# The first FFN of a macaron decoder layer in two token parts, each with seven products in place of eight

## The chip, the cores and the metric

The kernel runs on one core of a Trainium2 chip. The time is the device time of one execution in microseconds (us), the median of several runs; a profiled execution is recorded beside them. The engines are TensorE (PE in the profile; PEld is its weight load), VectorE (DVE), ScalarE (ACT), GpSimd (POOL) and SyncE (SP), which here issues the DMAs in one queue, in order.

## The reference

One decoder layer is computed on 1024 prompt tokens and 8 x 8 sample tokens, 1088 in all, with a model width of 1024. It is a macaron: half an FFN, a mixer (forgetting attention beside gated linear attention), half an FFN, each with a norm before and after.

```python
def rmsnorm(x, g):
    y = x32 * lax.rsqrt(jnp.mean(x32 * x32, axis=-1, keepdims=True) + NORM_EPS)
    return (y * g.astype(jnp.float32)).astype(x.dtype)

def swiglu(x, w_gu, w_down):
    gate, up = jnp.split(x @ w_gu, 2, axis=-1)
    return (jax.nn.silu(gate) * up) @ w_down

def macaron_half(x, g_pre, w_gu, w_down, g_post):
    return x + 0.5 * rmsnorm(swiglu(rmsnorm(x, g_pre), w_gu, w_down), g_post)
...
        hp = macaron_half(hp, ffn1_norm_pre[l], ffn1_w_gu[l], ffn1_w_down[l], ffn1_norm_post[l])
        fq, fk, fv, lf, gq, gk, gv, gg, la = project(rmsnorm(hp, mix_norm_pre[l]), w_in[l],
                                                     b_forget[l], w_gate_up[l], b_gate[l])
```

The FFN is 2752 wide. Behind the first FFN the result h is normalised again (`mix_norm_pre`) and multiplied by `w_in`: that is the projection.

## The kernel before, in words

**Layout.** Everything is kept transposed: 128 partitions are 128 of the model's or the FFN's features, and tokens run along the free dimension. The width of 1024 is 8 feature blocks (KB). Tokens come in four chunks, `CH` = (0,256), (256,256), (512,256), (768,320), written as (first, count); `MID` joins the first two to (0,512). HALF is 512, H1N the other 576.

**Precision.** A float32 operand is split in a high and a low part (`split`, L194 on ACT for the high part, L195 on DVE for the low one), and a product is three matmuls: high by high, high by low, low by high. Activations stand split in `ua` (first 512 tokens) and `ub` (last 576). A weight comes by DMA into a raw tile (`wr`, L118 in `Feed`, up to `ahead` of them split early), and its parts are `wh` and `wl`.

**The FFN.** Its 2752 columns are 22 blocks of 128 for gate and for up; block 0 is the odd one, whose half gate and half up share one weight. `GROUPS` cuts them in seven groups, [0,1], [2..5], [6..9], [10..13], [14..17], [18,19], [20,21], called G[0] to G[6]. For each block, gate and up are products over the chunks (`gemm`, L265, into PSUM tiles `mm`), DVE and ACT make silu(gate) x up and split it into `hh` and `hl`, and after a group `down` (L497) multiplies it back onto the 8 feature blocks of y, where DVE adds (L507) or, for G[0], ACT copies (L505). A group is planned as "first" (chunk after chunk as the norms come), "mid", or "final" (behind its downs stands the closing norm of each chunk, `after`). The first FFN is one `Part`, f1, over all 1088 tokens: G[0] first, G[1] to G[4] mid, and G[5] with G[6] final, once for the first 512 tokens and once for the others.

**Seven products.** The second FFN's second half (f3, 576 tokens) is planned with "sevens" already. Gate and up of one block are then seen as a product of 2 x 2 quarters: two halves of the 1024 features by two halves of the tokens, for the two weights. `seven` (L552) makes one product of half the features (4 x 3 matmuls) by half the tokens, and 7 of them give what 8 give in the plain way. It needs sums of weights, made by POOL (`Sums.load`: four DMAs L86, adds L89 and L94), sums of activations t1 to t4, made once by DVE and split, and additions of partial results on DVE (`job_seven`, L567 and L577). The sums of weights need scratch, given by `old`, and t1 to t4 need room, given by `room`.

**Norms.** `norm` (L351) sums squares (sq by ACT, ss by DVE or POOL, L275, L279, L281), adds over partitions on PE (`ncol`, L294), takes the power on DVE and POOL (`nv`, L324, L325), spreads it by a diagonal (`dg`, L336) and a matmul (`nrows`, L343), and multiplies: L382 for the closing norm, whose sum with x is L383 and is stored to `h1` by L388, and L405 for the next norm, split by L407 and L408 into `ua` or `ub`.

**Order.** A scheduler builds each engine's order from the program's. Each engine works in its own order, and so does SP's queue.

## Time and profile before

| what | value |
|---|---|
| median of three runs | 2387.77 us (2387.45 to 2388.52) |
| profiled execution, its own time | 2397.51 us |
| its span in the trace | 2395.8 us |
| mean granted TensorE clock | 0.984 |
| first product of the first FFN | 15.68 us |
| first product of the third chunk (`ub`) | 44.24 us |
| first product of the projection | 802.59 us |

The trace gives the start of every instruction in us, how long it took, its engine, its line, and the tiles that it writes and reads; in brackets stands how long the engine had been idle, and who ended that. A row of a window gives the stretch, its length, then for PE, PEld, DVE, ACT and POOL the busy time and, in brackets, the instructions; then the granted clock, the DMA share and GB/s. A closer look at the first FFN: from 200 to 300 us PE is busy for 100.00 us and DVE for 26.11.

### The profile page before, as it was taken

The page shows a single profiled execution, that of the slowest core. Times are in us where ns is not written, and L with a number is a line of the kernel's source. Part 1 is how long each engine was busy: PE and PEld are TensorE (multiplying, and loading weights), DVE is VectorE, ACT ScalarE, POOL GpSimd, SP SyncE. Part 2 cuts the span into 40 slices and gives each one's busy share as a digit, 9 for nine tenths or more (in the row PEclk, how much of TensorE's full clock was granted, in tenths as well). Part 3 has the DMA queues.
Part 4 walks back from the last instruction along what each step waited for, and adds up shares of the span by engine and source line. Part 5 has one row for each costly group of instructions (what it writes and reads, how often), then busy time and mean ns, then how long its engine had stood idle before and what let it go on. Part 6 is the DMA issues. An engine that isn't in the chain of part 4 may idle for free. (4 is left out here: it accounts for less than half of the span.)

```text
span 2395.8 us, 39346 instructions
## 1 busy us (share of the span) xinstructions
PE 2297.4 (96%) x15200; PEld 2041.2 (85%) x15200; DVE 1293.7 (54%) x2453; ACT 903.4 (38%) x1622; POOL 488.2 (20%) x514
## 2 busy tenths in 40 slices
PE   7999999999999999899998999998997999999997
PEld 6999999999989879899997666667786988999997
DVE  7223232232347774676465333339785696777765
ACT  5421211111134455755454222226565544334332
POOL 4000000000003230011124554531110224333402
PEclk9999999999999999999999999999998999999998
DMA  3211111111125576664458998766555544223212
GB/s 124 71 45 45 45 44 45 45 45 45 45 97 158 167 222 193 202 189 135 131 171 252 331 320 289 249 184 168 163 167 146 188 136 159 89 93 102 80 58 84
DMA packets 182267, 330.55 MB, mean 138 GB/s; under 512 B 25729, under 2 KB 101314, under 8 KB 182082
## 3 DMA queue, kind: packets, MB, share of 16 engines
q1 hardware_dynamic: 170418, 289.77, 38.8%
q0 software_dynamic: 11664, 38.28, 4.7%
q8 instruction: 120, 1.97, 0.3%
q14 instruction: 65, 0.53, 0.1%
HBM read 284.29 MB, written 43.69 MB: 137 GB/s over the span
## 5 line engine op out<-in xcount | busy, mean ns | idle before, releaser
L265 PE MATMUL mm<-ua,wh 128*128 128x512 f32 (+2 forms) x2288 | 635.4, 364 | 4.2 <-ACT ua L407 1.4
L265 PE MATMUL mm<-ub,wh 128*128 128x256 f32 (+2 forms) x2624 | 546.2, 303 | 10.7 <-ACT ub L194 8.3
L195 DVE TENSOR_TENSOR wl<-wr,wh 128x1024 fp32r<-128x1024 f32 (+1 forms) x258 | 312.0, 1210 | 337.7 <-ACT wh L194 325.7
L194 ACT CAST wh<-wr 128x1024 fp32r<-128x1024 f32 (+1 forms) x258 | 263.5, 1022 | 567.9 <-PE mm L265 196.8
L265 PEld LDWEIGHTS mm<-ua,wh 128*128 128x128 f32 (+1 forms) x2288 | 399.9, 191 | 80.7 <-issue 22.8
L265 PEld LDWEIGHTS mm<-ub,wh 128*128 128x128 f32 (+1 forms) x2624 | 428.3, 192 | 17.8 <-ACT ub L194 8.5
L265 PE MATMUL mm<-ua,wl 128*128 128x512 f32 (+1 forms) x1136 | 405.3, 358 | 1.2 <-DVE wl L195 1.2
L265 PE MATMUL mm<-ub,wl 128*128 128x256 f32 (+1 forms) x1296 | 386.8, 299 | 0.3 <-DVE wl L195 0.3
L497 PE MATMUL mm<-hl,wh 128*128 128x256 f32 (+2 forms) x1088 | 347.2, 320 | 0.8 <-DVE hl L195 0.5
L497 PE MATMUL mm<-hh,wh 128*128 128x256 f32 (+2 forms) x1040 | 337.1, 325 | 4.1 <-DVE y L507 2.0
L497 PE MATMUL mm<-hh,wl 128*128 128x256 f32 (+2 forms) x1040 | 331.9, 320 | 1.0 <-issue 1.0
L265 PEld LDWEIGHTS mm<-ub,wl 128*128 128x128 f32 x1296 | 248.4, 192 | 0.5 <-DVE wl L195 0.5
L265 PEld LDWEIGHTS mm<-ua,wl 128*128 128x128 f32 x1136 | 216.3, 191 | 33.3 <-DVE wl L195 2.3
L507 DVE TENSOR_TENSOR y<-y,mm 128x256 f32<-128x256 f32 (+2 forms) x272 | 130.1, 502 | 181.7 <-PE mm L497 169.5
L497 PEld LDWEIGHTS mm<-hl,wh 128*128 128x128 f32 x1088 | 205.9, 189 | 13.8 <-issue 2.0
L279 POOL TENSOR_TENSOR ss<-ss,sq 128x256 f32<-128x256 f32 (+1 forms) x46 | 46.1, 1003 | 836.9 <-ACT sq L275 836.3
L497 PEld LDWEIGHTS mm<-hh,wh 128*128 128x128 f32 x1040 | 196.0, 189 | 23.3 <-issue 6.5
L497 PEld LDWEIGHTS mm<-hh,wl 128*128 128x128 f32 x1040 | 196.4, 189 | 12.7 <-issue 1.1
L963 POOL DMA_INDIRECT pr<-in_cv,rows x128 | 131.1, 1024 | 119.5 <-PE po L1040 58.4
L435 DVE TENSOR_TENSOR sg<-mm,sg 128x256 f32<-128x256 f32 (+4 forms) x76 | 39.3, 517 | 134.5 <-PE mm L265 132.1
L194 ACT CAST hh<-sg 128x512 fp32r<-128x512 f32 (+2 forms) x92 | 47.0, 511 | 154.0 <-DVE sg L435 132.5
L552 PE MATMUL mm<-ub,wh 128*128 128x288 f32 x432 | 88.5, 298 | 4.1 <-ACT wh L194 4.1
(290 smaller groups left out, 3211.4 us busy)
## 6 DMA issues: line engine op xcount, KB each, us to landing
wr<-in_wgu SPq DMA_DIRECT2D x101, 512.0 KB
wr<-in_wd SPq DMA_DIRECT2D x60, 512.0 KB
pr<-in_ck SPq DMA_DIRECT2D x112, 256.0 KB
wr<-in_win SPq DMA_DIRECT2D x50, 512.0 KB
wr<-in_wout SPq DMA_DIRECT2D x32, 512.0 KB
wz<-in_wgu SPq DMA_DIRECT2D x36, 256.0 KB
h<-y SPq DMA_DIRECT2D x12, 512.0 KB
x<-h SPq DMA_DIRECT2D x24, 256.0 KB
```

What stands on the lines that cost most here:

```text
L194: self.keep(self.nc.scalar.copy(hi, src))
L195: self.keep(self.nc.vector.tensor_tensor(out=lo, in0=src, in1=hi.bitcast(F32), op=ALU.subtract))
L265: nc.tensor.matmul(out, a, x[:, k, o:o + n], start=(k == 0 and j == 0), stop=(k == KB - 1 and j == len(ops) - 1))
L279: (nc.gpsimd if odd else nc.vector).tensor_tensor(out=s, in0=s, in1=sq[:, :n], op=ALU.add)
L435: nc.vector.tensor_tensor(out=out, in0=u, in1=t, op=ALU.mult)
L497: nc.tensor.matmul(pds[e], a, b, start=(i == 0 and j == 0), stop=(i == len(g) - 1 and j == len(ops) - 1))
L507: nc.vector.tensor_tensor(out=yk, in0=yk, in1=pds[e], op=ALU.add)
L552: nc.tensor.matmul(ps, a, x, start=(k == 0 and j == 0), stop=(k == KB // 2 - 1 and j == len(ops) - 1))
L963: nc.gpsimd.indirect_dma_start(out=raw[:, i], out_offset=None, in_=A["ck" if kind == "K" else "cv"].rearrange("g p n -> (g p) n"), in_offs ...
```

## The change

The first FFN becomes two Parts, f1a over the first 512 tokens and f1b over the last 576, one behind the other, each over all weights, so every weight is loaded and split twice. In each, G[0] is "first", G[1] to G[5] (18 blocks) are "sevens", with products of 256 tokens in f1a and of 288 in f1b, and G[6] is "final". y is cut in `y0` and `y1`.

The scratch changes places. For f1a, `y1` holds the sums of weights and `ub` holds t1 to t4; `y1` gets its tokens only behind f1a's sevens (`next1`, one DMA of 128 x 8 x 576). For f1b, `y0` is the scratch and `ua` the room, so f1a's two closing norms must be done first; the normalised u of the first 512 tokens goes to DRAM (`u0`, `spill`) and is reloaded behind f1b's sevens and split into `ua` (`again`). `seven` takes all four banks of `mm`. During the first FFN one more weight is split early (`ahead`). The cached log-forget sums (`past_bias`) use `y0` as room, in two halves. f3 is built by the same function, `sums`, as f1a and f1b.

```diff
-        self.ahead = NW - 1
+        self.ahead = NW
...
+            if spill is not None:
+                if k % 4 == 3:
+                    nc.sync.dma_start(spill[:, k - 3:k + 1, c0:c0 + n], y[:, k - 3:k + 1, c0 - y0:c0 - y0 + n])
+                continue
...
-            ps = self.mm(n) if z.turn else self.px.tile([P, 512], F32, name=self.uid("mx"), tag="mx", bufs=1)[:, :n]
+            ps = self.mm(n) if z.turn or self.nmm > 3 else self.px.tile([P, 512], F32, name=self.uid("mx"), tag="mx", bufs=1)[:, :n]
...
-            uh, ul = self.ub
+            uh, ul, _ = self.at(f.b0)
...
-        y = F.tile([P, KB, T], F32, name="y")
+        y0 = F.tile([P, KB, HALF], F32, name="y0")
+        y1 = F.tile([P, KB, H1N], F32, name="y1")
         for k, m in ((0, 2), (2, 2), (4, 4)):
-            nc.sync.dma_start(y[:, k:k + m, :CH[0][1]], A["xT"][:, k:k + m, :CH[0][1]])
+            nc.sync.dma_start(y0[:, k:k + m, :CH[0][1]], A["xT"][:, k:k + m, :CH[0][1]])
...
+        def sums(f, room, old, first=lambda: None):
+
+            m, n = KB // 2 * f.n // 2, f.n // 2
+
+            def rooms():
+                cut = lambda r, i: [t[:, i * m:i * m + m].rearrange("p (k n) -> p k n", k=KB // 2) for t in r]
+                more = [f.H.tile([P, m], F32R, name=f"t4{i}", bufs=1) for i in range(2)] if f.n > HALF else room
+                return {f"t{i + 1}": cut(room, i) if i < 3 else cut(more, i % (4 if more is room else 3)) for i in range(4)}
+
+            def olds():
+                first()
+                y, h = old().rearrange("p k n -> p (k n)"), KB * P // 2
+                f.temps = [y[:, 4 * h + i * n:4 * h + i * n + n] for i in range(3)]
+                return y[:, :2 * h], y[:, 2 * h:3 * h], y[:, 3 * h:4 * h]
+            f.room, f.old = rooms, olds
 
...
+        def next1():
+            self.kept = False
+            nc.sync.dma_start(y1, A["xT"][:, :, HALF:])
+            for c in CH[2:]:
+                self.beside(self.norm(y1, HALF, *c, F, pre=0, key="f1"))
+
+        def again():
+
+            for k in range(0, KB, 2):
+                nc.sync.dma_start(y0[:, k:k + 2], self.u0[:, k:k + 2])
+                yield 2.0
+            for k in range(0, KB, 2):
+                s = slice(k, k + 2)
+                self.split(self.ua[0][:, s], self.ua[1][:, s], y0[:, s])
+                yield 2.0
+            self.ready.add(("p", CH[1][0]))
+
+        def next2():
+            self.kept = False
+            self.need(("u0", CH[1][0]))
+            self.beside(again(), True)
+
+        def plan1(chunks, then):
+            return [(G[0], chunks, "first")] + [(g, chunks, "sevens") for g in G[1:6]] + [(None, [([], then, 0)], "jobs"), (G[6], chunks, "final")]
+
+        f1a = Part(b0=0, n=HALF, y=y0, y0=0, H=F, N=F, tanh=False, firsts=CH[:2], first=first1, plan=plan1(MID[:1], next1),
+                   after=lambda c0, n, v: self.norm(y0, 0, c0, n, F, (1, A["xT"], self.h1), 2, v, "u0", self.u0))
+        f1b = Part(b0=HALF, n=H1N, y=y1, y0=HALF, H=F, N=F, tanh=False, firsts=CH[2:], first=lambda i: self.need(("f1", CH[2 + i][0])),
+                   plan=plan1(MID[1:], next2),
+                   after=lambda c0, n, v: self.norm(y1, HALF, c0, n, F, (1, A["xT"], self.h1), 2, v, "p"))
+        sums(f1a, flatb, lambda: y1)
+        sums(f1b, flata, lambda: y0, lambda: self.need(("u0", CH[1][0])))
+        jobs = self.ffn(A["wgu1"], A["wd1"], f1a) + self.ffn(A["wgu1"], A["wd1"], f1b)
+
+        def ahead(n):
+            self.feed.ahead = n
+        jobs.append(([], lambda: ahead(NW - 1), 0))
 
```

Line numbers behind the change are 4 higher for the lines named (L497 becomes L501, L552 L556, L507 L511, L567 L571, L408 L412, L435 L439). The listed order of the five engines is the same from the projection on. Three places are different ahead of it.

POOL, at the start. `nv` is the power of a norm, `ss` a sum of squares, `ua1` the low part of the first tokens' u, `y1`, `wx` and `wz` hold weights and their sums. Before:

```order
L408 TENSOR_TENSOR ua1_99<-y_111,ua0_98 128x256 x4
L279 TENSOR_TENSOR ss_32_224<-ss_32_224,sq_34_229 128x256
L279 TENSOR_TENSOR ss_32_224<-ss_32_224,sq_36_235 128x256
L325 TENSOR_TENSOR nv_40_248<-nv_40_248,mhalf_67 128x2
L279 TENSOR_TENSOR ss_47_367<-ss_47_367,sq_49_372 128x256
```

And after the change:

```order
L412 TENSOR_TENSOR ua1_100<-y0_112,ua0_99 128x256 x4
L279 TENSOR_TENSOR ss_32_224<-ss_32_224,sq_34_229 128x256
L279 TENSOR_TENSOR ss_32_224<-ss_32_224,sq_36_235 128x256
L89 TENSOR_TENSOR y1_113<-y1_113,wz_57_466 128x512
L89 TENSOR_TENSOR wx_56_465<-y1_113,wx_56_465 128x512
L89 TENSOR_TENSOR y1_113<-wx_56_465,y1_113 128x512
L94 TENSOR_TENSOR y1_113<-wz_57_466,wx_56_465 128x512
L325 TENSOR_TENSOR nv_40_248<-nv_40_248,mhalf_67 128x2
```

Between the sums of squares of the second chunk and its power `nv_40` four sums of weights stand now.

DVE, where the first down weights are split. `sg` and `hl` are the hidden block, `wl_47`, `wl_52`, `wl_54` are low parts of down weights, `wt_58` is the odd block's share of one, L630 makes t1 to t4 in `y0`, and `ub1` is their low part. Before, behind the same hidden block:

```order
L435 TENSOR_TENSOR sg_27_176<-mm_44_314,sg_27_176 128x256
L279 TENSOR_TENSOR ss_46_365<-ss_46_365,sq_52_381 128x256
L281 TENSOR_TENSOR ss_46_365<-ss_46_365,ss_47_367 128x256
L195 TENSOR_TENSOR hl_25_174<-sg_27_176,hh_24_173 128x256
L279 TENSOR_TENSOR ss_46_365<-ss_46_365,sq_53_385 128x256
L435 TENSOR_TENSOR sg_26_175<-mm_45_358,sg_26_175 64x256
L324 TENSOR_SCALAR nv_55_391<-ncol2_54_388 128x2
L279 TENSOR_TENSOR ss_61_508<-ss_61_508,sq_63_512 128x320
L472 TENSOR_TENSOR hl_23_172<-sg_26_175,hh_22_171 64x256
L336 TENSOR_TENSOR dg_56_415<-ident_60,nv_55_391 128x256
```

And after the change:

```order
L195 TENSOR_TENSOR wl_47_387<-wr_20_169,wh_46_386 128x512
L439 TENSOR_TENSOR sg_26_177<-mm_45_358,sg_26_177 64x256
L195 TENSOR_TENSOR ub1_105<-y0_112,ub0_104 128x512 x2
L476 TENSOR_TENSOR hl_23_174<-sg_26_177,hh_22_173 64x256
L195 TENSOR_TENSOR wl_52_456<-wr_21_171,wh_51_455 128x512
L630 TENSOR_TENSOR y0_112<-y0_112 128x2x256 x2
L195 TENSOR_TENSOR wl_54_460<-wr_48_390,wh_53_459 128x512
L195 TENSOR_TENSOR ub1_105<-y0_112,ub0_104 128x512 x2
L630 TENSOR_TENSOR y0_112<-y0_112 128x2x256 x3
L195 TENSOR_TENSOR ub1_105<-y0_112,ub0_104 128x512 x3
L630 TENSOR_TENSOR y0_112<-y0_112 128x2x256
L644 CAST wt_58_492<-wl_47_387 64x256
```

Before, the norm of the third chunk followed the hidden block; now the sums of activations and their splits do, with the down weights between them, and `wt_58` behind.

SP, at the end of f1a. `x` are the tokens to be added, `h1` the stored result, `wr` raw weights. Before, in this place of the end of the first 512 tokens:

```order
L118 DMA wr_613_5866<-in_wgu1 128x1024
L118 DMA wr_628_5960<-in_wgu1 128x1024
L368 DMA x_621_5918<-in_xT 128x2x256
L368 DMA x_624_5944<-in_xT 128x2x256
L388 DMA h1_86<-y_111 128x4x256
L368 DMA x_655_6221<-in_xT 128x2x256
L388 DMA h1_86<-y_111 128x4x256
L118 DMA wr_638_6043<-in_wgu1 128x1024
L368 DMA x_656_6223<-in_xT 128x2x256
```

And after the change:

```order
L408 DMA u0_86<-y0_112 128x4x256 x2
L368 DMA x_698_4398<-in_xT 128x2x256
L368 DMA x_701_4411<-in_xT 128x2x256
L388 DMA h1_87<-y0_112 128x4x256
L368 DMA x_1324_8600<-in_xT 128x2x256
L388 DMA h1_87<-y0_112 128x4x256
L368 DMA x_1325_8602<-in_xT 128x2x256
L118 DMA wr_811_5046<-in_wd1 128x1024
L408 DMA u0_86<-y0_112 128x4x256 x2
L86 DMA y0_112<-in_wgu1 128x512
L1640 DMA y0_112<-u0_86 128x1024
L86 DMA y0_112<-in_wgu1 128x512
```

The spills `u0` stand between the stores of `h1` and the first load of weights (L86) into `y0`, and a first reload (L1640) stands behind that.

58 lines of the change are left out of this document (22 added, 36 removed).

## The prediction

> **What bounds the kernel now.** I read the first lines of the page, then the busy time by windows over the first FFN, then the timeline row by row where the change acts.
>
> ```profile
> span 2395.8 us, 39346 instructions
> PE 2297.4 (96%) x15200; PEld 2041.2 (85%) x15200; DVE 1293.7 (54%) x2453; ACT 903.4 (38%) x1622; POOL 488.2 (20%) x514
> 70.00:660.00 590.00, 590.00 (x3576) 539.98 (x3576) 162.87 (x246) 107.26 (x172) 0.00 (x0) 1.00 0.15 47
> 802.59 0.63 PE L265 MATMUL mm<-ua,wh 128*128 128x512 f32 x2
> ```
>
> TensorE (PE) is busy in 96% of the span. From 70 to 660 us, the bulk of the first FFN, it is busy for all 590.00 us at a granted clock of 1.00, while VectorE (DVE) works 162.87 us and the DMA engines are at 0.15 of their time. So this stage is bound by PE alone, and fewer matmul columns shorten it one for one, as long as nobody else becomes late. The last row is the first product of the projection: the first FFN ends for PE at 802.59. In the listed order of instructions everything behind that point is the same in both kernels, so the whole question is where this row comes to stand.
>
> **What a matmul costs.** Matmuls overlap, so I take the distance of starts, not durations.
>
> ```profile
> 659.00 0.61 PE L265 MATMUL mm<-ua,wh 128*128 128x512 f32 x2
> 659.68 0.61 PE L265 MATMUL mm<-ua,wh 128*128 128x512 f32 x2
> 590.45 0.40 PE L265 MATMUL mm<-ub,wh 128*128 128x256 f32 x2
> 591.17 0.40 PE L265 MATMUL mm<-ub,wh 128*128 128x256 f32 x2
> 2337.40 0.46 PE L265 MATMUL mm<-ub,wh 128*128 128x320 f32 x2
> 2337.84 0.45 PE L265 MATMUL mm<-ub,wh 128*128 128x320 f32 x2
> 2100.41 0.43 PE L552 MATMUL mm<-ua,wh 128*128 128x288 f32 x2
> 2105.20 0.43 PE L552 MATMUL mm<-ub,wh 128*128 128x288 f32 x2
> ```
>
> 512 columns: 3 matmuls in 0.68 us, 0.2267 each. 256: 6 in 0.72, 0.120. 320: 3 in 0.44, 0.1467. 288, in the second FFN, which has the 7 products already: 36 in 4.79, 0.133. One block of gate and up takes 48 matmuls in each of three chunks before: 48 x (0.2267 + 0.120 + 0.1467) = 23.68 us. After it takes 7 products of 4 x 3 matmuls, once with 256 and once with 288 columns: 84 x (0.120 + 0.133) = 21.25 us. That is 2.43 us less a block, **43.7 us for 18 blocks**. The down products keep their columns.
>
> The Trainium skill speaks against this: "TensorE: Matmul & The Clock Gate", section "Back-to-back issue gap", gives a sustained spacing of about 81 ns at 128 columns and 131 ns at 512, so that halved products would hardly be cheaper. By a straight line between these figures (an estimate from that page) a block would cost 16.1 us before and 16.8 after, a loss of about 12 us in place of the 43.7 gained. The rows above differ (226.7 ns at 512, 120 at 256), and the measurement decides.
>
> **The start.** Here the order changes most.
>
> ```profile
> 23.35 0.74 POOL L279 TENSOR_TENSOR ss<-ss,sq 128x256 f32<-128x256 f32 x1 [0.90 <-ACT sq L275]
> 28.25 0.71 POOL L325 TENSOR_TENSOR nv<-nv,mhalf 128x2 f32<-128x2 f32 x1 [4.17 <-DVE nv L324]
> 28.99 0.95 DVE L336 TENSOR_TENSOR dg<-ident,nv 128x256 f32<-128x256 f32 x1 [0.82 <-POOL nv L325]
> 31.26 0.87 DVE L405 SCALAR_TENSOR_TENSOR y<-y,gain,nrows 128x256 f32<-128x256 f32 x2 [0.98 <-PE nrows L343]
> 36.04 0.41 DVE L435 TENSOR_TENSOR sg<-mm,sg 128x256 f32<-128x256 f32 x1
> 44.24 0.68 PE L265 MATMUL mm<-ub,wh 128*128 128x256 f32 x4
> 66.68 0.40 PE L497 MATMUL mm<-hh,wt 128*128 128x512 f32 x1
> 69.00 0.28 PE L497 MATMUL mm<-hh,wt 128*128 128x256 f32 x1
> 1996.80 0.68 DVE L195 TENSOR_TENSOR wl<-wr,wh 128x512 fp32r<-128x512 f32 x1
> 1997.40 0.42 DVE L383 TENSOR_TENSOR y<-y,x 128x256 f32<-128x256 f32 x1
> 2010.27 1.26 POOL L89 TENSOR_TENSOR y<-wx,y 128x512 f32<-128x512 f32 x1
> ```
>
> GpSimd's (POOL's) power for the second chunk's norm runs at 28.25, 4.17 us after its last work. In the new order four weight sums of 1.26 us stand ahead of it, and they wait for weights: some 3 us late, and with it DVE's normalisation at 31.26 and its row of 36.04. Behind that row DVE now has, ahead of the split of the first down weights (`wt_58`) and of the second half of the hidden block (`hl_25`), 8 subtractions L630 and 8 splits of 512 elements (0.60 each, 1996.80 to 1997.40: 9.6 us) and some 4.5 us of others. 36.04 + 3 + 14.1 gives 53.1, and I take 53.3. Before, PE had the third and fourth chunk of G[0] to multiply at 44.24; that work now lies in the second part, so PE waits 9.1 us. A wait of 4.1 us at 2013.88 (below) cost 2.9 us of half clock on top; I add as much. **Start: 12.0**, with 3.5 (the sums come in time and DVE is ready soon after PE) and 15 as ends.
>
> **Blocks of the first part.** DVE per block stands next to PE.
>
> ```profile
> 2107.49 1.22 DVE L195 TENSOR_TENSOR wl<-wx,wh 128x1024 fp32r<-128x1024 f32 x1
> 2108.63 0.44 DVE L567 TENSOR_TENSOR sg<-y,mm 128x288 f32<-128x288 f32 x1
> 2119.02 1.21 DVE L195 TENSOR_TENSOR wl<-wx,wh 128x1024 fp32r<-128x1024 f32 x1
> ```
>
> One block of 288 takes DVE 11.53 us from one `wx` split to the next, against 84 x 0.133 = 11.17 on PE. With 256 columns the splits of weights stay as long, and only the rows on tokens shrink: about 10.5 us of DVE against 84 x 0.120 = 10.08 of PE. 18 x 0.42 = 7.6; the down products between the groups, where DVE has little to do, give part back. **I take 3**, between 0 and 13 (10.8 a block).
>
> **The last group of the first part.** y1 was scratch for the sums, so its 2.36 MB are loaded only when the last seven is done, ahead of the next weights on SyncE's (SP's) queue.
>
> ```profile
> 20.00:25.00 5.00, 4.99 (x42) 4.78 (x40) 4.10 (x7) 2.20 (x6) 3.19 (x4) 1.00 1.08 361
> ```
>
> At 361 GB/s that is 6.5 us, and 1.5 more for the first gate weights of 512 KB, some 2 of latency and 2.2 for their casts: 12.2 against the 11.2 us of down products (48 x 0.2325, the spacing of ten 512-column downs from 66.68 to 69.00) that hide it. Then DVE has 30 us of work in its listed rows from the norms of y1 to the last down addition, plus two chains of waits, beside 33 us of PE. **I take 6**, between 2 and 9.5.
>
> **From the first part to the second.** The first seven of the second part needs y0 as scratch, and y0 must first be normalised, stored and spilled. The second FFN shows the same place without the second norm and the spill:
>
> ```profile
> 1975.25 0.40 PE L265 MATMUL mm<-ub,wh 128*128 128x256 f32 x2
> 1977.55 0.42 DVE L279 TENSOR_TENSOR ss<-ss,sq 128x256 f32<-128x256 f32 x1
> 1977.89 0.75 DVE L195 TENSOR_TENSOR t<-y,t 128x576 fp32r<-128x576 f32 x1
> 1978.56 0.42 DVE L281 TENSOR_TENSOR ss<-ss,ss 128x256 f32<-128x256 f32 x1
> 1997.74 1.26 DVE L382 SCALAR_TENSOR_TENSOR y<-y,gain,nrows 128x256 f32<-128x256 f32 x3
> 1998.91 0.42 DVE L383 TENSOR_TENSOR y<-y,x 128x256 f32<-128x256 f32 x1
> 2004.81 0.34 SPq L86 DMA_DIRECT2D y<-in_wgu  x1
> 2009.04 1.27 POOL L89 TENSOR_TENSOR y<-y,wz 128x512 f32<-128x512 f32 x1 [6.49 <-DMA y<-in_wgu]
> 2013.88 0.85 PE L552 MATMUL mm<-ub,wh 128*128 128x288 f32 x2 [4.12 <-ACT wh L194]
> 2015.71 0.68 PE L552 MATMUL mm<-ub,wh 128*128 128x288 f32 x2
> 2016.19 0.44 PE L552 MATMUL mm<-ub,wl 128*128 128x288 f32 x1
> 2014.00:2337.50 323.50, 321.22 (x2377) 319.21 (x2378) 240.23 (x345) 119.99 (x160) 105.70 (x69) 0.99 0.27 85
> ```
>
> PE's work in this stage is 72 x (0.120 + 0.1467) for G[0] and 40 x 0.2667 for its downs, 29.9 us. In the second FFN the stage took 38.6 us (1975.25 to 2013.88). In the new order DVE has, from the last down addition to the last row that feeds the spill, 32 scalar_tensor_tensor of 256 (0.39 by 1997.74 to 1998.91, three in 1.17: 12.5), 31 tensor_tensor of 256 (0.34: 10.5), 16 of 576 (0.67: 10.7) and 6.5 us of others: 40.2 us. Three chains of power, diagonal and row sum stop it for 1.8 us each (0.82 + 0.98, in front of 28.99 and 31.26): 45.6. The load of weights into y0 may go when the spill of the first four blocks has landed, some 0.9 us later, 46.5. From there 4.2 us to POOL (2004.81 to 2009.04) and 4.8 to the first seven: 55.5 against 29.9 of PE work. PE waits 25.6 us, and the first products run at half clock (0.24 in place of 0.133, 2015.71 to 2016.19) for 2.9 more. **Handover: 28.5**, between 12 (as in the second FFN, 38.6 - 29.9 + 2.9) and 32.
>
> **The second part** is the second FFN's half again: its window of 323.5 us holds 18 x 11.17 + 18 x 24 x 0.2667 = 316.3 us of products and the 2.9 of half clock; 4.4 remain. Its end has four reloads and splits of u, 0.5.
>
> **The sum.** In the kernel before, from 66.68, the downs of G[0], 20 blocks and their downs are 40 x 0.499 + 20 x 23.68 + 480 x 0.499 = 733.1 us of products (0.499 = 0.2325 + 0.120 + 0.1467); they took 735.9, so 2.8 were lost, and 3.2 more from 44.24 to 66.68 (22.4 us for 19.2 of products). These 6.0 go, and the terms above come in their place: -43.7 - 6.0 + 12.0 + 3 + 6 + 28.5 + 4.4 + 0.5 = **+4.7 us**. The projection would start near 807. The profiled execution took 2397.51 us, 1.7 over its span, and 0.4% more than the median of 2387.77 (2387.45 to 2388.52). 2402.2 / 2397.51 x 2387.77 = 2392.4; the y0 reload that SP's order places among the first sums adds 1.4 us at 361 GB/s for its 512 KB, of which I count half, 0.7: **2393**.
>
> **Rivals.** (1) *The handover is no longer than the second FFN's*, because ScalarE and POOL take squares and additions early and DVE's splits of t fall into its waits: 41.5 us with the half clock in place of 58.4, 17 us less: 2376. For it speaks that the 16 operations of 576 elements are not needed by the spill; against it that DVE works in its listed order, and those rows stand between. (2) *DVE sets the pace of the first part* (slower): each block above 10.08 us on DVE costs 18 times the excess. At 10.8 us, the 11.53 of above less little, it is 13 in place of 3: 2403. It decides from 10.35 a block on; the 0.36 us by which DVE exceeds PE at 288 speak for it, the downs that give back against it. (3) *The start costs 3.5 only*, 8.5 less: 2384.5; for it, that the rows on the critical side are short, against it, that 16 rows stand ahead. (4) *Short matmuls carry a price of their own.* 0.2267 - 0.120 over 256 columns is 0.417 ns a column and leaves 13 ns a matmul; 24 more matmuls a block would eat the 43.7 us only at 101 ns more each: 2436. The 288 rows (0.133, where 0.417 x 288 + 13 gives 133 ns) exclude it nearly. The skill's rule of above is this rival. (5) *PE isn't shortened*, the blocks not taking the short way: the listed order shows 84 matmuls a block, so near nothing.
>
> **How the numbers follow.** The forecast (2388 to 2398) 0.42, rival 1 0.22, rival 2 0.16, rival 3 0.17, rival 4 0.01, rival 5 0.02. The range takes rival 1 and rival 2 with their spread: 2374 to 2407; about 0.15 stays out. A measurement of this kernel tells 0.2%, 4.8 us, from no change: 2383 to 2392.5. Faster holds rival 1 and a part of 3: 0.27. Same holds the lower half of the forecast, most of 3 and rival 5: 0.33. Slower holds the rest, 0.40.
>
> **What the new profile would show.** Right: L265 and seven rows of 0.120 and 0.133 in the first FFN; PE's first wait of 7 us or more near 46 on DVE; one wait of 20 to 28 us near 370 to 430 with SP's load into y0 late; the projection's first product near 807. Wrong: that product before 795 (then the handover or the start is cheap) or after 815 (then DVE stretches the blocks, and PE's waits lie in every block).

## The result, and the profile after

| | before | after |
|---|---|---|
| median of 7 runs, us | 2388.52 (2387.29 to 2395.91) | 2409.82 (2401.16 to 2410.88) |
| profiled execution, its own time | 2397.51 | 2410.29 |
| its span | 2395.8 | 2408.5 |
| first product of the projection | 802.59 | 829.79 |
| from there to the end of the span | 1593.2 | 1578.7 |

The change made the kernel slower: 1.0079 of the time before, 95% interval 1.0063 to 1.0095. The forecast was 2393 in a range of 2374 to 2407, so the direction was right and the loss four times too small.

The first FFN ends 27.2 us later, where 4.7 were forecast. The instructions behind that point are the same in both kernels, and yet they took 1578.7 to 1593.2 us; over all the profiled kernels below it was 1576 to 1596, with no order that follows the change. So the start of the projection is what the experiments compare. The medians differ by 21.3 us; the 6 us between that and 27.2 are less than this spread, and were not traced further.

From the first lines of the page of the kernel after:

```profile
span 2408.5 us, 41672 instructions
PE 2270.2 (94%) x15584; PEld 2039.4 (85%) x15584; DVE 1616.2 (67%) x2881; ACT 1041.9 (43%) x1786; POOL 693.6 (29%) x650
```

And from its windows (stretch, length, busy time and count of PE, PEld, DVE, ACT and POOL, granted clock, DMA share, GB/s):

```profile
70.00:340.00 270.00, 262.06 (x1798) 240.79 (x1797) 210.09 (x275) 107.60 (x143) 97.91 (x64) 1.00 0.31 94
357.21:404.82 47.61, 41.28 (x213) 34.89 (x213) 37.32 (x71) 24.33 (x53) 16.32 (x19) 0.90 0.28 84
404.82:468.49 63.67, 41.65 (x258) 39.86 (x257) 45.52 (x100) 28.41 (x64) 18.96 (x20) 0.79 0.47 145
```

PE is busy 27 us less than before, and the span is longer. DVE works 322 us more. Between 70 and 340 us, where PE was busy without a gap, it now idles 8 us in 270, and DVE is busy for 210 of them. The last two rows are the first part's last group and the handover: PE is idle for 6.3 and 22 us and its granted clock is 0.90 and 0.79.

PE's timeline after, the rows at which a stage begins or PE waited:

```profile
51.08 0.76 PE L501 MATMUL mm<-hh,wt 128*128 128x512 f32 x1 [7.62 <-DVE wt L644]
61.88 0.40 PE L556 MATMUL mm<-ua,wh 128*128 128x256 f32 x2
...
102.65 0.40 PE L501 MATMUL mm<-hh,wh 128*128 128x512 f32 x1
127.34 0.40 PE L556 MATMUL mm<-ua,wh 128*128 128x256 f32 x2
...
305.45 0.74 PE L501 MATMUL mm<-hh,wh 128*128 128x512 f32 x2 [1.57 <-ACT hh L583]
357.21 0.72 PE L265 MATMUL mm<-ua,wh 128*128 128x512 f32 x2 [1.52 <-ACT wh L194]
398.44 0.36 PE L501 MATMUL mm<-hh,wh 128*128 128x256 f32 x1 [2.38 <-DVE y L511]
404.82 0.63 PE L265 MATMUL mm<-ub,wh 128*128 128x256 f32 x2
430.04 0.99 PE L294 MATMUL ncol<-ones,ss 128*128 128x2 f32 x4 [4.13 <-DVE ss L279]
438.60 1.20 PE L343 MATMUL nrows<-dg,ones 128*128 128x128 f32 x4 [4.41 <-DVE dg L336]
448.61 0.64 PE L501 MATMUL mm<-hl,wh 128*128 128x320 f32 x1 [5.06 <-DVE hl L195]
468.49 0.85 PE L556 MATMUL mm<-ub,wh 128*128 128x288 f32 x2 [5.47 <-ACT wh L194]
515.64 0.28 PE L501 MATMUL mm<-hh,wh 128*128 128x256 f32 x1
540.94 0.43 PE L556 MATMUL mm<-ub,wh 128*128 128x288 f32 x2
585.52 0.28 PE L501 MATMUL mm<-hh,wh 128*128 128x256 f32 x1
829.79 0.70 PE L265 MATMUL mm<-ua,wh 128*128 128x512 f32 x2 [0.62 <-DVE y L511]
```

The first part's sevens begin at 61.88, four blocks take 40.77 us (to 102.65), their downs 24.69 (to 127.34). The last group begins at 357.21, the second part at 404.82, its first seven at 468.49, and four of its blocks take 44.58 (540.94 to 585.52), 11.15 a block. Against the products alone this gives, by the terms of the prediction:

| term | predicted, us | measured, us | how |
|---|---|---|---|
| start | 12.0 | 8.3 | 61.88 - (44.24 + 9.3) |
| blocks of the first part | 3 | 11.9 | 357.21 - 61.88 - 1.52, less 18 x 10.08 + 432 x 0.2325 |
| last group of the first part | 6 | 16.1 | 404.82 - 357.21 + 1.52, less 33.0 |
| handover | 28.5 | 36.4 | 468.49 - 404.82 - 29.9, and 2.6 of low clock behind (515.64 - 468.49 against 44.58) |
| second part and its end | 4.9 | 4.1 | 829.79 - 468.49 - 2.6, less 354.6 (316.3, and the last group) |
| sum, of unrounded terms | 54.4 | 76.9 | 22.5 more: 4.7 becomes 27.2 |

The saving in the blocks is there, and three terms were too small.

### The profile page after: what moved, and what is told of

It is laid out like the page before. It is cut to its first block, busy times and chain, and to the rows that moved or that the text cites. A ratio compares the mean times of both kernels' runs of the same rounds, so it can differ in the third digit from the quotient of the medians.

```text
span 2408.5 us, 41672 instructions
## 1 busy us (share of the span) xinstructions
PE 2270.2 (94%) x15584; PEld 2039.4 (85%) x15584; DVE 1616.2 (67%) x2881; ACT 1041.9 (43%) x1786; POOL 693.6 (29%) x650
## 5 line engine op out<-in xcount | busy, mean ns | idle before, releaser
L265 PE MATMUL mm<-ua,wh 128*128 128x512 f32 (+2 forms) x1712 | 461.8, 358 | 9.1 <-ACT wh L194 5.8
L501 PE MATMUL mm<-hl,wh 128*128 128x320 f32 (+2 forms) x1072 | 349.5, 327 | 7.3 <-DVE hl L195 5.8
L501 PE MATMUL mm<-hh,wh 128*128 128x256 f32 (+2 forms) x1024 | 335.9, 331 | 15.5 <-ACT hh L583 6.4
L501 PE MATMUL mm<-hh,wl 128*128 128x256 f32 (+2 forms) x1024 | 332.2, 325 | 0.9 <-DVE wl L195 0.9
L265 PE MATMUL mm<-ub,wh 128*128 128x320 f32 (+1 forms) x1472 | 312.0, 307 | 10.1 <-ACT ub L194 7.9
L265 PE MATMUL mm<-ua,wl 128*128 128x512 f32 (+1 forms) x848 | 296.3, 351 | 2.2 <-DVE wl L195 2.2
L556 PE MATMUL mm<-ub,wh 128*128 128x288 f32 (+1 forms) x1440 | 281.4, 291 | 8.4 <-ACT wh L194 8.4
L265 PEld LDWEIGHTS mm<-ub,wh 128*128 128x128 f32 x1472 | 239.3, 193 | 13.9 <-ACT ub L194 8.1
L556 PEld LDWEIGHTS mm<-ub,wh 128*128 128x128 f32 x1440 | 229.9, 191 | 8.9 <-ACT wh L194 8.9
L511 DVE TENSOR_TENSOR y<-y,mm 128x256 f32<-128x256 f32 (+2 forms) x296 | 142.1, 505 | 137.4 <-PE mm L501 136.4
L501 PEld LDWEIGHTS mm<-hh,wh 128*128 128x128 f32 x1024 | 194.5, 191 | 38.2 <-ACT hh L583 8.6
L556 PE MATMUL mm<-ua,wh 128*128 128x288 f32 (+1 forms) x1152 | 226.2, 293 | 0.0
L501 PEld LDWEIGHTS mm<-hl,wh 128*128 128x128 f32 x1072 | 206.7, 193 | 21.7 <-DVE hl L195 6.7
L265 PE MATMUL mm<-ub,wl 128*128 128x256 f32 (+1 forms) x720 | 215.7, 300 | 0.5 <-DVE wl L195 0.5
L89 POOL TENSOR_TENSOR y<-y,wz 128x512 f32<-128x512 f32 x54 | 71.8, 1329 | 490.5 <-DVE wl L195 473.5
L556 PE MATMUL mm<-ub,wl 128*128 128x288 f32 (+1 forms) x720 | 210.1, 292 | 0.0
L501 PEld LDWEIGHTS mm<-hh,wl 128*128 128x128 f32 x1024 | 195.7, 191 | 15.0 <-DVE wl L195 2.6
L556 PEld LDWEIGHTS mm<-ua,wh 128*128 128x128 f32 x1152 | 185.0, 191 | 0.5
```

The costliest lines, as they stand in the source:

```text
L89: nc.gpsimd.tensor_tensor(out=out, in0=a, in1=b, op=op)
L265: nc.tensor.matmul(out, a, x[:, k, o:o + n], start=(k == 0 and j == 0), stop=(k == KB - 1 and j == len(ops) - 1))
L501: nc.tensor.matmul(pds[e], a, b, start=(i == 0 and j == 0), stop=(i == len(g) - 1 and j == len(ops) - 1))
L511: nc.vector.tensor_tensor(out=yk, in0=yk, in1=pds[e], op=ALU.add)
L556: nc.tensor.matmul(ps, a, x, start=(k == 0 and j == 0), stop=(k == KB // 2 - 1 and j == len(ops) - 1))
```

## The experiments

Each kernel is the one after with the edit that is shown, or with two of these edits (parted, end_one_norm, half_end_fill, end_fill). The table gathers the starts on PE (from the timelines, in us); rest is from the projection to the end of the span. end_fill and end_fill_timed are one kernel, and their projections start 1.9 us apart: a difference of that size between two rows says nothing.

| kernel | second part | its first seven | projection | rest |
|---|---|---|---|---|
| before | | | 802.59 | 1593.2 |
| after | 404.82 | 468.49 | 829.79 | 1578.7 |
| a_only | 404.97 | none | 825.11 | 1595.6 |
| b_only | 392.40 | 451.58 | 812.86 | 1591.6 |
| parted | 393.39 | none | 811.93 | 1591.3 |
| fill_handover | 403.73 | 497.69 | 818.97 | 1589.1 |
| end_both | 390.85 | 449.71 | 810.49 | 1587.1 |
| one_norm | 403.79 | 452.72 | 812.96 | 1581.7 |
| end_one_norm | 390.22 | 433.58 | 794.21 | 1582.4 |
| pool_low | 403.80 | 466.60 | 827.22 | 1576.1 |
| half_end | 403.78 | 445.69 | 806.54 | 1582.1 |
| half_end_fill | 401.91 | 479.35 | 800.86 | 1588.4 |
| end_fill | 391.59 | 476.36 | 797.65 | 1580.0 |
| end_fill_timed | 390.12 | 474.49 | 795.76 | 1581.7 |

### What each part's seven products give: a_only, b_only, parted

a_only, the second part plain:

```diff
-                   after=lambda c0, n, v: self.norm(y0, 0, c0, n, F, (1, A["xT"], self.h1), 2, v, "u0", self.u0))
+                   after=lambda c0, n, v: self.norm(y0, 0, c0, n, F, (1, A["xT"], self.h1), 2, v, "p"))
...
-                   plan=plan1(MID[1:], next2),
+                   plan=[(G[0], MID[1:], "first")] + [(g, MID[1:], "mid") for g in G[1:5]] + [(G[5] + G[6], MID[1:], "final")],
...
-        sums(f1b, flata, lambda: y0, lambda: self.need(("u0", CH[1][0])))
```

> Measure: start of the projection's first product (before 802.6, after 829.8). Here the second part (576 tokens) takes the plain 8 products, so nothing of it needs y0 as scratch and u is not spilled. Theory (the handover's 36 us are the wait for that scratch): the first part ends near 405 as before, no wait of PE over 3 us behind it, 18 x (12.8 - 11.15) = 30 us more products; the projection starts near 820 to 823. Rival (the handover is bound by the norms themselves, whoever needs them): the wait stays and the projection starts near 855.

b_only, the first part plain, with y1 loaded and normalised from the start:

```diff
+                nc.sync.dma_start(y1, A["xT"][:, :, HALF:])
...
+            if i == 1:
+                for c in CH[2:]:
+                    self.beside(self.norm(y1, HALF, *c, F, pre=0, key="f1"))
...
-        f1a = Part(b0=0, n=HALF, y=y0, y0=0, H=F, N=F, tanh=False, firsts=CH[:2], first=first1, plan=plan1(MID[:1], next1),
+        f1a = Part(b0=0, n=HALF, y=y0, y0=0, H=F, N=F, tanh=False, firsts=CH[:2], first=first1, plan=[(G[0], MID[:1], "first")] + [(g, MID[:1], "mid") for g in G[1:5]] + [(G[5] + G[6], MID[:1], "final")],
...
-        sums(f1a, flatb, lambda: y1)
```

> Here the first part (512 tokens) takes the plain 8 products and y1 is loaded at the start; the second part stays with 7. Theory (the sevens of the first part save 18 x 0.7 = 12 us and cost 8 at the start, 12 in its blocks and downs, 16 in its last group): the first part ends near 382 to 386 in place of 404.8, the handover stays near 64 us, the projection starts near 808 to 811. Rival (these losses come from the parting in two, not from the sevens): the first part ends near 415 and the projection starts near 840.

parted has both edits.

> Two parts, but both with the plain 8 products, y1 loaded at the start, no scratch, no spill. Theory (the losses add up part by part): a_only and b_only share nothing of their sevens, so the first part ends near 392 as in b_only and the second takes 420 as in a_only; the projection starts near 812, 10 behind the kernel before, and from there the sevens of the first part cost 12 and those of the second 5. Rival (both parts' sevens only lose by being together): it starts near 803 to 806, and the sevens cost 25.

The rows of a_only, from the timeline of PE:

```profile
428.77 0.36 PE L501 MATMUL mm<-hh,wt 128*128 128x256 f32 x1 [2.45 <-DVE wt L644]
825.11 0.63 PE L265 MATMUL mm<-ua,wh 128*128 128x512 f32 x2
```

Without the need for y0 the second part has one wait over 1 us, 2.45. So the norms themselves stop nobody; the handover's 36 us come with the need for the scratch. They come with more than that: a_only also leaves out the sums of the second part's activations and their splits, 12.5 us of VectorE in the handover of the kernel after. The projection starts at 825.11, 2 us behind the theory's range and 30 ahead of the rival's figure. The second part takes 420.1 us plain and 425.0 with seven products: its blocks win 18 x 1.65 = 30 us (51.18 for four plain blocks, 44.58 for four with seven) and the handover takes more than that.

b_only's first part ends at 392.40, not at the 382 to 386 expected: the start costs it 9 us without any sevens (its blocks begin at 62.85, against 44.24 + 9.3). It has y1's norms at the start, as the kernel before has them, but no third and fourth chunk of products to stand beside them. That point went to the rival; for the rest the first part's sevens cost 12.4 us (404.82 less 392.40) where they were to save 12. The projection starts at 812.86, near the theory's 808 to 811 and far from the rival's 840, and the handover, with y1 normalised early, is 59.2. parted's projection starts at 811.93, where b_only's first part and a_only's second put it (392.4 + 420.1 = 812.5): the losses add, as the theory has it. Against parted, the parting costs 9.3 of the 27.2 us, the first part's sevens 11.4 (404.82 to 393.39), and the second's 6.4 (425.0 to 418.5).

### The handover: fill_handover, one_norm, end_one_norm

```diff
-                   plan=plan1(MID[1:], next2),
+                   plan=[(G[0], MID[1:], "first"), (G[6], MID[1:], "mid")] + [(g, MID[1:], "sevens") for g in G[1:5]] + [(None, [([], next2, 0)], "jobs"), (G[5], MID[1:], "final")],
```

> The second part's last group [20,21] is moved to its front as plain products, before the sevens, and [18,19] becomes the plain last group: 38 us of products stand between the first group and the first seven, and 2 blocks lose the 7 products (3.3 us). Theory (the handover is a wait for the scratch y0 with a length of its own, about 64 us): PE has 68 us of products there, waits 0 to 5 us, and the projection starts near 797 to 803. Rival (VectorE's work sets it, and the moved group adds 16 us to it): the first seven moves back by as much, PE waits 11 us or more, the projection starts at 808 to 815.

It starts the projection at 818.97, behind both ranges. PE's waits from the second part's begin to its first seven, by engine and line waited for (total, times, longest):

```profile
PE nrows L343 <- DVE dg L336: 6.4, 2, 4.4
PE ncol L294 <- DVE ss L279: 4.3, 1, 4.3
PE mm L501 <- DVE hl L195: 3.0, 1, 3.0
PE mm L501 <- DVE wt L644: 2.5, 1, 2.5
```

The first seven waits for nothing now, but 16 us of waits lie ahead of the filled-in work: PE's own steps of the norms (ncol, nrows) stand in its queue inside the first group, and the hidden block and down weights come late from DVE. Neither theory had PE itself held up by the norms. Every one of these waits is for DVE, so the handover is two things: a wait for scratch, and before it a congestion on DVE.

```diff
+                if spill is not None:
+                    for k in (0, 4):
+                        nc.sync.dma_start(spill[:, k:k + 4, c0:c0 + n], y[:, k:k + 4, c0 - y0:c0 - y0 + n])
...
-                   after=lambda c0, n, v: self.norm(y0, 0, c0, n, F, (1, A["xT"], self.h1), 2, v, "u0", self.u0))
+                   after=lambda c0, n, v: self.norm(y0, 0, c0, n, F, (1, A["xT"], self.h1), None, v, "u0", self.u0))
```

> The kernel after the change without the second norm of the first 512 tokens: y0 is spilled as it stands behind the closing norm, so the outputs are computed from an unnormalised u. Stage: from the second part's first product (404.8 in the kernel after) to its first seven (468.5), 63.7 us. Theory (a chain of VectorE's work and the norms' waits for PE and GpSimd ends it, and the second norm holds 20 us of that chain): the stage takes 41 to 46 us. Rival (stores, spills and the load into y0 behind them end it, and the norm lies beside them): it takes 55 us or more.

The stage took 48.9 us (403.79 to 452.72): 14.8 less, between the two ranges of the expectation and nearer the theory's. The second norm stands on the chain; it is worth 14.8 us there, where the theory has 18 to 23.

> end_both and one_norm together: y1's norms are out of the handover's way, and the second norm of the first 512 tokens is left out, so y0 is spilled unnormalised and the outputs come from an unnormalised u. The stage from the second part's first product to its first seven took 63.7 us in the kernel after, 58.9 in end_both, 48.9 in one_norm and 38.6 at the same place of the second FFN. Theory (the two causes add): 44 us, and the 5 left over the second FFN's stage are the spill that the load into y0 waits for. Rival (the two share their waits): 47 us or more.

```profile
433.58 0.85 PE L559 MATMUL mm<-ub,wh 128*128 128x288 f32 x2 [6.84 <-ACT wh L194]
```

43.4 us (390.22 to 433.58): the causes add. The 63.7 us are 38.6 as in the second FFN, 14.8 for the second norm, 4.8 for what end_both (below) moves out of the stage, and 5.5 that were not taken apart; that they are the spill was not tested. By the expectation these 4.8 us are y1's norms; but in the kernel after the last row of these on DVE is at 398.54, ahead of the stage. What end_both moves out of it are the 16 rows behind them, the sums of the second part's activations (L630) and their splits: 12.5 us of DVE, between 407.7 and 442.3 in the kernel after, and between 351.9 and 369.6, before the stage, in end_both.

### The last group of the first part: end_both

```diff
-        f1a = Part(b0=0, n=HALF, y=y0, y0=0, H=F, N=F, tanh=False, firsts=CH[:2], first=first1, plan=plan1(MID[:1], next1),
+        f1a = Part(b0=0, n=HALF, y=y0, y0=0, H=F, N=F, tanh=False, firsts=CH[:2], first=first1, plan=[(G[0], MID[:1], "first")] + [(g, MID[:1], "sevens") for g in G[1:5]] + [(None, [([], next1, 0)], "jobs"), (G[5] + G[6], MID[:1], "final")],
```

> The first part ends with the plain groups [18,19] and [20,21] in place of [20,21] alone, so y1 is loaded and normalised beside 77 us of products in place of 33; 2 blocks lose the 7 products (1.5 us). Theory (the last group's loss of 16 us is VectorE's norm of y1 that does not fit beside it): the loss falls to 5 or less, the projection starts near 819 to 821. Rival (it is a chain of waits between PE, VectorE and the power of the norm, as long whatever stands beside it): the loss stays and the projection starts near 831.

From the windows of end_both, the two groups' gate and up, and their downs:

```profile
321.04:366.94 45.90, 45.90 (x213) 38.28 (x212) 37.68 (x61) 23.22 (x41) 10.57 (x12) 1.00 0.27 84
366.94:390.85 23.91, 23.13 (x194) 22.73 (x192) 17.20 (x32) 10.31 (x21) 4.78 (x6) 1.00 0.28 94
```

69.8 us against 65.9 of products (the expectation has 77, which the two groups are not): the loss falls from 16.1 to 3.9, PE has hardly a gap, and its clock is 1.00. And the handover behind it is 58.9 in place of 63.7. The projection starts 19.3 us earlier, twice what was expected. What happened in the kernel after shows in DVE's timeline there:

```profile
384.29 1.01 DVE L405 SCALAR_TENSOR_TENSOR y<-y,gain,nrows 128x320 f32<-128x320 f32 x2 [4.66 <-PE nrows L343]
...
392.58 1.41 DVE L511 TENSOR_TENSOR y<-y,mm 128x256 f32<-128x256 f32 x4
...
396.96 1.00 DVE L405 SCALAR_TENSOR_TENSOR y<-y,gain,nrows 128x320 f32<-128x320 f32 x2
397.88 0.74 DVE L511 TENSOR_TENSOR y<-y,mm 128x256 f32<-128x256 f32 x2
```

DVE waited 4.66 us for PE's `nrows`, which stood behind gemms in PE's order, part of them at half clock (the last section); then its late norm of y1 lay among the additions L511 that empty PSUM, and PE waited 2.38 us at 398.44 for one of them. Either engine had the time, but they waited for each other in turn.

### The blocks of the first part: pool_low, half_end

```diff
-            low = lambda c: self.keep(nc.vector.tensor_tensor(out=hl[:, c], in0=t[:, c], in1=hh[:, c].bitcast(F32), op=ALU.subtract))
...
+            sub = lambda e, c: e.tensor_tensor(out=hl[:, c], in0=t[:, c], in1=hh[:, c].bitcast(F32), op=ALU.subtract)
+            low = lambda c: self.keep(sub(nc.vector, c)) if last or f.n > HALF else sub(nc.gpsimd, c)
```

> The kernel after with one operation of 512 elements a block (the low part of the hidden block, not of a group's last block) moved from VectorE to GpSimd in the first part. Theory (in the first part VectorE, 91% busy over the sevens, runs behind PE and makes it wait where the down products begin): a group's downs fall from 24.7 to 23 us or less and 4 blocks from 40.77 to 40.4, so the first part's last group begins 6 to 9 us earlier, near 349 to 351 in place of 357.2. Rival (the wait there is the chain of additions, silu, product and casts of the last block, as long on an idle VectorE): it stays near 357, or later if the sums of weights on GpSimd now wait.

From the timeline of PE in pool_low:

```profile
304.29 0.50 PE L501 MATMUL mm<-hh,wh 128*128 128x512 f32 x1 [1.77 <-ACT hh L583]
356.84 0.73 PE L265 MATMUL mm<-ua,wh 128*128 128x512 f32 x2 [2.08 <-ACT wh L194]
```

Four blocks fall to 40.31 (257.82 to 298.13), but the downs stay at 24.7, the wait at `hh` is 1.77, and the last group begins at 356.84. That is the rival's number, but not yet its cause, for the edit did not relieve VectorE. The windows over the same four blocks, in the kernel after and in pool_low:

```profile
258.29:299.05 40.76, 40.56 (x338) 40.35 (x337) 37.03 (x48) 19.02 (x25) 21.44 (x14) 1.00 0.32 97
257.82:298.13 40.31, 40.31 (x338) 40.31 (x336) 36.58 (x45) 18.95 (x25) 26.72 (x17) 1.00 0.30 99
```

VectorE lost three operations of 0.87 us, and is still busy for 36.58 us in place of 37.03: other operations of its own became longer beside GpSimd's new ones (`wl<-y` of 1024 elements 1.65 us in place of 1.21, `wl<-wx` 1.40 in place of 1.21).

What settles it is end_both. Behind its last group of sevens come plain products, so GpSimd has no sums of weights to make beside that group's last block. VectorE's rows there, first in the kernel after, then in end_both, where the last row is PE's first down product:

```profile
277.07 1.21 DVE L195 TENSOR_TENSOR wl<-wx,wh 128x1024 fp32r<-128x1024 f32 x1
...
287.85 1.21 DVE L195 TENSOR_TENSOR wl<-wx,wh 128x1024 fp32r<-128x1024 f32 x1
291.11 2.20 DVE L195 TENSOR_TENSOR wl<-wz,wh 128x1024 fp32r<-128x1024 f32 x1
294.94 1.79 DVE L195 TENSOR_TENSOR wl<-y,wh 128x512 fp32r<-128x512 f32 x1
299.76 0.41 DVE L571 TENSOR_TENSOR sg<-y,mm 128x256 f32<-128x256 f32 x1
...
287.44 1.21 DVE L195 TENSOR_TENSOR wl<-wx,wh 128x1024 fp32r<-128x1024 f32 x1
290.70 1.21 DVE L195 TENSOR_TENSOR wl<-wz,wh 128x1024 fp32r<-128x1024 f32 x1
292.77 0.68 DVE L195 TENSOR_TENSOR wl<-y,wh 128x512 fp32r<-128x512 f32 x1
296.93 0.41 DVE L571 TENSOR_TENSOR sg<-y,mm 128x256 f32<-128x256 f32 x1
298.64 0.40 PE L501 MATMUL mm<-hh,wh 128*128 128x512 f32 x1
```

The order is the same, but from the split `wl<-wx` to the last block's first addition VectorE takes 11.91 us in the kernel after and 9.49 in end_both. There the wait at `hh` is gone, and the downs take 22.40 us (298.64 to 321.04), the price of their products (96 x 0.2325 = 22.3). end_one_norm, end_fill and end_fill_timed show the same at this place. So VectorE's lateness is the cause after all: beside GpSimd's sums a block takes it 10.78 us (277.07 to 287.85), PE 10.19, and PE pays for the lag at the group's end.

half_end gives the downs pieces of 256 tokens, so that they wait for half a hidden block, and ends the first part chunk by chunk:

```diff
-        f1a = Part(b0=0, n=HALF, y=y0, y0=0, H=F, N=F, tanh=False, firsts=CH[:2], first=first1, plan=plan1(MID[:1], next1),
+        f1a = Part(b0=0, n=HALF, y=y0, y0=0, H=F, N=F, tanh=False, firsts=CH[:2], first=first1, plan=[(G[0], MID[:1], "first")] + [(g, CH[:2], "sevens") for g in G[1:5]] + [(None, [([], next1, 0)], "jobs")] + [(G[5] + G[6], [c], "final") for c in CH[:2]],
```

> The first part ends with [18,19] and [20,21] as plain products, first for tokens 0 to 255 and then for 256 to 511, and the down products of its sevens run in two pieces of 256. Theory: the norms of y1 and both norms of the first 256 tokens lie beside the second piece's 33 us of products, so only one chunk's norms are left for the handover: from the second part's first product to its first seven it takes 38 to 45 us in place of 63.7; a group's downs take 22.5 us in place of 24.7, since they wait for a half of the hidden block only; 2.5 us more for products of 256; the projection starts at 790 to 797, before the 802.6 of the kernel before, and the time is 6 to 12 us under the kernel before. Rival (a handover has 58 us whatever stands ahead, as in end_both): the projection starts near 805 to 810 and the time is not under the kernel before.

The wait at `hh` is gone, and the downs still take 24.0 to 24.6 us, not 22.5. The first row is a wait that takes its place, the second the first seven of the second part:

```profile
103.04 0.39 PE L501 MATMUL mm<-hh,wl 128*128 128x256 f32 x1 [0.71 <-DVE wl L195]
...
445.69 0.76 PE L556 MATMUL mm<-ub,wh 128*128 128x288 f32 x2 [4.27 <-ACT wh L194]
```

The handover is 41.9 us (403.78 to 445.69), as the theory has it and against the rival's 58. But the last groups, whose weights are now loaded and split twice, take 84.9 us against 69.8 in end_both, where 2.5 more were expected, and the projection starts at 806.54, inside the rival's range for another reason than the rival's. The windows of their downs:

```profile
344.88:362.23 17.35, 14.28 (x98) 13.79 (x97) 14.89 (x24) 10.24 (x20) 6.43 (x6) 0.80 0.47 140
386.13:403.78 17.65, 15.55 (x106) 15.11 (x105) 16.48 (x31) 10.37 (x19) 6.09 (x7) 0.81 0.74 233
```

DVE is busy for 15 and 16.5 of 17.5 us and PE's clock falls to 0.80. The time is 2389.43 (12 runs), 1.0002 of the kernel before (0.9989 to 1.0015): no difference.

### Versions: half_end_fill, end_fill

> half_end and fill_handover together. Theory (in half_end the handover still holds 5 to 12 us of waits of PE for its scratch, and the fill covers them for 3.3 us): the projection starts 2 to 9 us ahead of half_end. Rival (half_end leaves no such wait): it starts 3 us behind half_end.

The projection starts at 800.86, 5.7 ahead of half_end. The time is 2388.81 (12 runs), 1.0004 (0.9993 to 1.0015): the same as before.

> end_both and fill_handover together. In end_both PE waits 12.4 us for the first seven and loses some 2 more at a low clock. Theory (PE's waits ahead of the scratch are small once y1's norms are out of the way): the fill saves these 14 us for 3.3: the projection starts near 799 to 801. Rival (as in fill_handover, where PE waits for the norms inside the first group): it starts at 805 or later.

797.65, a little better than expected: with y1's norms and the sums of activations out of the way PE waits 8.7 us ahead of the sevens, where fill_handover had 16.

> The kernel of end_fill, timed. Its projection started at 797.7, 4.9 before that of the kernel before. Theory (what happens behind that start is the same): the time is 3 to 7 us under the kernel before, ratio 0.997 to 0.999. Rival (the part behind the start takes back what the first part gains): ratio 1.000 to 1.002.

The time is 2381.41 (12 runs, 2376.18 to 2387.11), 0.9973 of the kernel before, interval 0.9962 to 0.9984. This version, with 16 of the 22 blocks in seven products in either part, is 0.27% faster than the kernel before. Against the kernel after it was not timed side by side; the two ratios put it 1% ahead.

## Why the prediction was wrong

**The blocks (right).** Four blocks of 288 take 44.58 us, 11.15 each where 11.17 were forecast; four of 256 take 40.77, 10.19 each against 10.08. So the 43.7 us are there, less 2. The Trainium skill's figures in "TensorE: Matmul & The Clock Gate", section "Back-to-back issue gap", by which halved products would hardly be cheaper, are not borne out by these rows either.

**The start (12.0: near, 8.3).** PE's wait on the odd down weight is there, 7.62 us at 51.08, where 9.1 were forecast, and the low clock behind it cost 1.5 (10.8 us for 9.3 of downs) in place of 2.9. The 16 rows of sums and what stands with them took what was forecast, 14.3 us (from 36.36 to `wt` at 50.64) where 14.1 were. The 3 us for the four sums of weights ahead of them were wrong: GpSimd's power ran at 29.09 in place of 28.25, and VectorE's row at 36.36 in place of 36.04. But these sums are not all that can make the start late. parted has none of them, and its first group's downs stand from 42.48 to 63.11, 20.6 us for 9.3, with y1's norms in their place. In either case the two chunks of products that hid such work in the kernel before stand elsewhere; what the start would be with neither, no run shows.

**The blocks' stalls ("I take 3": wrong, 11.9).** The step put VectorE at about 10.5 us a block against 10.08 of PE, and let the downs between the groups give part of it back. It takes 10.78, since its splits and products take up to 1.1 us longer while GpSimd makes the sums (2.20 in place of 1.21, 1.79 in place of 0.68), and nothing is given back: the downs need the last block's hidden values, VectorE comes late to them, and PE loses 2.4 us at the end of each group of four. That is 9.5 of the 11.9 us; 2 are the blocks themselves. Where GpSimd has no sums to make, end_both's last group of sevens, the loss at the group's end is gone. In the second part the first piece of downs needs half a hidden block and its groups' downs take 25.3 us for 25.6 of products; giving the first part such pieces (half_end) brought 0.1 to 0.7 us of the 2.4, since VectorE's split of the first down weight is then late.

**The last group ("I take 6": wrong, 16.1).** The step added up VectorE's work, 30 us beside 33 of PE, and called it hidden. The sum was right (37 us busy with the part ahead of it, in 47.6) and the conclusion wrong: the norm goes back and forth between PE, GpSimd and VectorE, each in its own order, and each hop waits behind other work. end_both, with 65.9 us of products beside the same norms, brought it to 3.9. Of the 16.1 us, PE's idle time is 7.9 (6.3 in the window and 1.52 ahead of it); the clock of 0.90 over 47.6 us is worth some 4.8 more (an estimate, 0.10 x 47.6), a cost that the step did not have.

**The handover (28.5: wrong, 36.4).** The order was as forecast: last row of the norm, the load into y0, the sums, the first seven. On DVE, SP and POOL of the kernel after, and the window from the last down addition to the end of that row:

```profile
456.56 1.65 DVE L405 SCALAR_TENSOR_TENSOR y<-y,gain,nrows 128x256 f32<-128x256 f32 x4
459.72 0.34 SPq L86 DMA_DIRECT2D y<-in_wgu  x1
463.66 1.26 POOL L89 TENSOR_TENSOR y<-y,wz 128x512 f32<-128x512 f32 x1 [10.51 <-DMA y<-in_wgu]
405.09:458.24 53.15, 36.59 (x222) 35.07 (x222) 44.94 (x97) 23.91 (x54) 14.21 (x16) 0.77 0.45 138
```

From the load to POOL 3.9 us and from there to PE 4.8, as in the second FFN. The load stands 1.5 us behind the row where 0.9 was taken, a figure for which the prediction shows no row. What failed is the term "45.6": the row ends at 458.2, 53.1 us behind the last down addition (405.1). The larger half of the 7.5 us is VectorE's work: it was busy for 44.9 us where 40.2 were forecast. Its waits for the steps of the norms on PE, GpSimd and ScalarE and for `x` came to 7.5 in all, where three chains were priced at 5.4. PE's waits at `ncol` and `nrows` inside the first group (4.13 and 4.41) are waits for this VectorE. With those at `hl` and at the first seven (5.06 and 5.47) they stand in place of the one wait of 20 to 28 us that was to be the sign of a right forecast. The stage becomes shorter in three ways: without the second norm (14.8), with the sums of activations made earlier (4.8), and, in half_end, with part of these sums and the first chunk's norms beside the last groups (41.9 in place of 63.7).

**The rivals.** Rival 1 (as short as the second FFN's) would need the second norm and the sums of the second part's activations out of the stage: end_one_norm, without either, is at 43.4. Rival 2 (VectorE sets the pace of the first part) had the sign, the mechanism and nearly the price of its term, 13 where 11.9 were measured at 10.78 us a block; but PE pays at the groups' ends and not in every block, and the term is 8.9 of the 22.5 us that were missing. Rival 3 put the start at 3.5, where 8.3 were measured. And the range failed in its build: it moved one term at a time, where three terms, all of them VectorE and PE waiting for each other at a change of stage, went the same way together. That the direction was right is partly luck: the sum stood 4.7 us from no change, less than the error of each of these three terms, and all three erred to the slow side.

## What to carry to other kernels

Where a stage is bound by one engine, a saving on that engine is real, but each place at which its work changes (a group's end, a part's end) then has less work to hide what stands there; count these places and price each by what it waits for. An engine beside it that takes a little longer for each block (10.78 us against 10.19 here) shows that at such a place, and its price has to be read from rows with the same neighbours at work; moving an operation to a neighbour that slows it (pool_low) relieves little. A norm that passes from engine to engine is a chain whose length is set by what stands ahead of it in each queue; 33 us of products were too few to hide 30 us of it here, 66 were enough. If a saving costs scratch that is still in use, keep as much of the plain work as fills the wait: 16 blocks of the cheaper kind in each part, with the wait filled, beat 18 with the wait open.

## What the runs showed of the hardware

Some operations of VectorE take longer while GpSimd adds. The split `wl<-wz` of 128x1024 takes 2.20 us beside GpSimd's sums and 1.21 without them, the split `wl<-y` of 128x512 1.79 and 0.68, the product of 128x512 (L581) 1.45 and 0.68; GpSimd's own addition L89 takes up to 2.27 in place of 1.26. VectorE's additions of a PSUM tile (L571, 128x256) are at 0.41 in both cases.

PE's clock can fall soon after a short wait. In the kernel after PE waits 1.14 us for a sum of squares (376.48), the only gap between 365.33 and there, and some 2 us later its matmuls of 512 take twice as long for 3 us; by the windows:

```profile
377.00:379.00 2.00, 2.00 (x10) 1.69 (x10) 0.70 (x3) 1.12 (x2) 0.87 (x1) 0.86 0.03 8
379.00:381.00 2.00, 2.00 (x6) 1.51 (x6) 0.62 (x2) 0.00 (x0) 0.00 (x0) 0.50 0.15 27
381.00:383.00 2.00, 2.00 (x9) 1.59 (x8) 0.00 (x0) 0.00 (x0) 0.00 (x0) 0.79 0.28 104
```

Waits of 1.57 us, as at 305.45, show no such drop: the window of 20 us around that one has a clock of 1.00. In fill_handover it is the other way round at the same place of the kernel: the clock is 0.50 from 361 to 363 us, behind a wait of 1.65 (357.89), where the kernel after shows 1.00 behind one of 1.52 (357.21), and it stays at 1.00 behind a wait of 0.92 at 378.35. The Trainium skill, "TensorE: Matmul & The Clock Gate", section "HAM oscillation — how this bites in real kernels", puts the limit for a gap at about 3.4 us; here drops stood behind waits of 1.14 and 1.65 us, and none behind others of 1.5 to 1.6. That the wait alone makes the drop is not shown, and what decides was not tested.
